# SSD decays: per-head exponentials with a bias on ScalarE and a mask added by Pool, in place of subtractions on VectorE

## The chip, the cores and the metric

One core of one Trainium2 chip runs the whole program. The metric is the device time of one execution in microseconds (us). The engines are named as the profile names them: PE (TensorE, with PEld its weight loads), DVE (VectorE), ACT (ScalarE), POOL (GpSimd) and SP (SyncE, which issues the DMAs).

## The reference, cut to what matters

One layer of a hybrid decoder: an LRU group, a dilated attention group and a Mamba-2 SSD group share an input projection and an output projection. The prompt has 2048 tokens, the sample group 8 sequences of 4 tokens. The change lies in the SSD group, in the decay of a chunk of Q = 128 tokens:

```python
cum = jnp.cumsum(dt * A, axis=2)
seg = cum[:, :, :, None, :] - cum[:, :, None, :, :]
causal = jnp.tril(jnp.ones((Q, Q), dtype=bool))
decay = jnp.exp(jnp.where(causal[None, None, :, :, None], seg, -jnp.inf))
...
scores = jnp.einsum('bcihn,bcjhn->bcijh', Ch, Bh) * decay
y_diag = jnp.einsum('bcijh,bcjhp->bcihp', scores, xdt)
```

There are 16 heads in 2 groups, so 16 chunks times 2 groups of 8 heads, each head with a 128 x 128 matrix of decays.

## The kernel before, in words

The program runs in stages: the input projections, the convolutions, the state of the samples, the attention of the prompt, and last the SSD chunks of the prompt together with the output projection. In this last stage `out_chunk(c)` issues the matmuls of the output projection of chunk c (tile `ops`, L82 to L84, 96 of them for a chunk), and between them the generator `ssd_part(c)` advances the SSD work of a later chunk by steps. The code gives a rough order; the framework's scheduler then fixes the order of the instructions on every engine when the program is built, and at run time each engine goes through its list strictly in order and waits at semaphores.

The SSD work of a chunk has a part for each group g of 8 heads, called here the g=0 part and the g=1 part:

- `ssd_open` (once for a chunk) multiplies B and C on PE (`gp`, L700), and DVE multiplies that with the 0/1 triangle (`gm`, L703). Entries outside the triangle are zero in `gm`.
- `ssd_decay` takes the tile `sg` (128 x 8 heads x 128), which a DMA fills with the row sums `cum` of the chunk, the same in all partitions (L680). There is one such buffer, so the DMA of the next part starts when the matmuls `yd` (L1291) have read this one. ACT first makes `ecB`, exp of the rows, in two pieces (L726). Then DVE subtracts for each head the column sum and caps at 0 (L728, eight instructions of 128 x 128), ACT takes the exponential of all of it (L730, one of 128 x 1024), and DVE multiplies by `gm` (L731, 128 x 1024).
- `ssd_x` turns x on PE (`tpx`, L741), and DVE scales it to `xdt` (L744). POOL multiplies x by D in place (`xb`, L1285) and makes `xte` (L750).
- PE then does `yd` from `sg` and `xdt` (L1291) and `yo` from the state (L1296). DVE sums up y (L1304 to L1307).
- `group_norm`: ACT squares y (`sq`, L757), POOL adds twice (L758, L759), PE sums over partitions (`rs`, L762), ACT makes `rB` (L764, L765), DVE scales y (L766); ACT rounds it to `sh` (L1328) and DVE takes the rest `sl` (L1329). These two are weights of later `ops` matmuls.
- Chunk 0 is prepared ahead, under the last attention unit (`ssd_early`, with buffers `c_`), and chunk 16 is the samples.

ACT and DVE also turn the output chunk into weights (`mh`, L1440, and `ml`, L1441) and finish its rows (`jk`, L1494, `rstd`, `ot`, L1508 and L1509).

Of the kernel before, what the change touches and what calls it, by code (L numbers as in the profile page):

```python
# [8 lines left out]
F32 = mybir.dt.float32  # L9
F32R = mybir.dt.float32r  # L10
AF = mybir.ActivationFunctionType
OP = mybir.AluOpType
# [14 lines left out]
NEG = -1.0e30  # L27
# [5 lines left out]
def tile_hybrid_step(ctx: ExitStack, tc: tile.TileContext, A):  # L33
    nc = tc.nc
    act, dve, pool, pe, sp = nc.scalar, nc.vector, nc.gpsimd, nc.tensor, nc.sync
# [26 lines left out]
    cum = const.tile([128, 17, 16], F32, name="cum")  # L62
# [38 lines left out]
    def softplus_of(pl, out, x, shape, tag):  # L101

        u = pl.tile(shape, F32, tag=tag + "u", name="sp_u")
        dve.tensor_scalar(out=u, in0=x, scalar1=-1.0, scalar2=None, op0=OP.mult)
        dve.tensor_tensor(out=u, in0=u, in1=x, op=OP.min)
        act.activation(out=u, in_=u, func=AF.Exp)
        log1p_of(pl, out, u, shape, tag)
        dve.scalar_tensor_tensor(out=out, in0=x, scalar=0.0, in1=out, op0=OP.max, op1=OP.add)
# [11 lines left out]
    def big(name, n=1024, dt=F32R):  # L120

        if n > 1024:
            return slab.tile([128, n], dt, tag="C", name=name, bufs=8)
        return slab.tile([128, n], dt, tag="A", name=name)
# [327 lines left out]
    with tc.tile_pool(name="dtp", bufs=1) as dp:  # L452

        xx = dp.tile([128, 17, 16], F32, name="xx")
        dve.tensor_tensor(out=xx, in0=dtT, in1=bB[:, None, :].to_broadcast([128, 17, 16]), op=OP.add)
        softplus_of(dp, dtT.rearrange("p c h -> p (c h)"), xx.rearrange("p c h -> p (c h)"), [128, 272], "dt")
        act.activation(out=aB, in_=aB, func=AF.Exp)
        dve.scalar_tensor_tensor(out=xx, in0=dtT, scalar=-1.0, in1=aB[:, None, :].to_broadcast([128, 17, 16]),
                                 op0=OP.mult, op1=OP.mult)
        tr = dp.tile([128, 2, 128], F32, name="tr")  # L460
        sp.dma_start(out=tr[:, 0], in_=A["c_tri"])
        pool.memset(tr[:, 1], 1.0)
        trs = dp.tile([NS, 2, NS], F32, name="trs")
        sp.dma_start(out=trs[:, 0], in_=A["c_tris"])
        sp.dma_start(out=trs[:, 1], in_=A["c_ones"])
        pool.memset(cum[:, 16], 0.0)
        pool.memset(dec[:, 16], 0.0)
        foldT = dp.tile([NS, 128], F32, name="foldT")
        sp.dma_start(out=foldT, in_=A["c_foldT"])
        selh = dp.tile([16, 8, 128], F32, name="selh")  # L470
        sp.dma_start(out=selh, in_=A["c_selh"])
        se = dp.tile([NS, 2, 16], F32, name="se")
        rws = dp.tile([16, 64], F32, name="rws")


        def sums():
            for j, dst in ((0, cum), (1, dec)):
                ps = psA.tile([128, 512], F32, tag="mm", name="cps")
                pe.matmul(ps[:, :256], lhsT=tr[:, j], rhs=xx[:, 0:16].rearrange("p c h -> p (c h)"), start=True, stop=True)
                dve.tensor_copy(out=dst[:, 0:16].rearrange("p c h -> p (c h)"), in_=ps[:, :256])  # L480
                ps = psA.tile([128, 512], F32, tag="mm", name="cps")
                pe.matmul(ps[:NS, :16], lhsT=trs[:, j], rhs=xx[:NS, 16], start=True, stop=True)
                dve.tensor_copy(out=dst[:NS, 16], in_=ps[:NS, :16])
            dve.tensor_tensor(out=tend, in0=dec, in1=cum, op=OP.subtract)
            act.activation(out=tend, in_=tend, func=AF.Exp)
            act.activation(out=dec, in_=dec, func=AF.Exp)
            act.activation(out=se[:, 0], in_=cum[:NS, 16], func=AF.Exp)
            dve.tensor_tensor(out=se[:, 1], in0=tend[:NS, 16], in1=dtT[:NS, 16], op=OP.mult)
            later.append(turn_sums)

        def turn_sums():
            ps = psA.tile([128, 512], F32, tag="mm", name="sps")
            pe.matmul(ps[:, :32], lhsT=foldT, rhs=se.rearrange("t a h -> t (a h)"), start=True, stop=True)
            dve.tensor_copy(out=srep.rearrange("p a h -> p (a h)"), in_=ps[:, :32])
            tp = psT.tile([128, 4, 128], F32, tag="tp", name="tp")
            rw = dp.tile([128, 2, 128], F32, name="rw")
            for g in range(2):
                pe.transpose(tp[:, g], cum[:, 8 * g:8 * g + 8].rearrange("p c h -> p (c h)"), ident)
            pe.transpose(tp[:16, 2, :NS], cum[:NS, 16], ident[:NS, :NS])
            pe.transpose(tp[:16, 3, :NS], dec[:NS, 16], ident[:NS, :NS])  # L500
            dve.tensor_copy(out=rw, in_=tp[:, 0:2])
            sp.dma_start(out=d_cum.rearrange("(g p) t -> p g t", p=128), in_=rw)
            dve.tensor_copy(out=rws.rearrange("p (a t) -> p a t", a=2), in_=tp[:16, 2:4, :NS])
            sp.dma_start(out=d_cums, in_=rws[:, :NS])
            later.append(spread)

        def spread():
            tq = psT.tile([128, 4, 128], F32, tag="tp", name="tq")
            for m in range(8):
                pe.matmul(tq[:, 0, 8 * m:8 * m + 8], lhsT=selh[:, m], rhs=rws[:, NS:64:NL], start=(m == 0), stop=(m == 7),  # L510
                          skip_group_check=True)
            dve.tensor_copy(out=decs.rearrange("p m b -> p (m b)"), in_=tq[:, 0, :64])

        later.append(lambda: later.append(sums))
        q_tile(1)
# [203 lines left out]
    def ssd_decay(c, g, ck, gm, ecB=None):  # L719

        n = TT[c][1]
        sg = load_sg(ck, c, g)
        if ecB is not None:
            for e in range(2):
                pt_ = slice(64 * e, 64 * e + 64)
                act.activation(out=ecB[pt_], in_=sg[pt_].rearrange("p (m e) t -> p e m t", e=2)[:, e], func=AF.Exp)  # L726
        for h in range(8):
            dve.tensor_scalar(out=sg[:n, h], in0=sg[:n, h], scalar1=cum[:n, c, 8 * g + h:8 * g + h + 1],  # L728
                              scalar2=0.0, op0=OP.subtract, op1=OP.min)
        act.activation(out=sg[:n], in_=sg[:n], func=AF.Exp)  # L730
        dve.tensor_tensor(out=sg[:n], in0=sg[:n], in1=gm[:n, g:g + 1].to_broadcast([n, 8, n]), op=OP.mult)  # L731
        return sg

# [505 lines left out]
    late = {}  # L1239

    def ssd_early():

        def piece(t, o, m, n=128):
            return t[:, o:o + m * n].rearrange("p (m t) -> p m t", m=m)

        c_ = [big(f"c0{i}", XC, F32) for i in range(8)]
        bc, tri0 = piece(c_[0], 0, 4), c_[7][:, 512:640]
        sp.dma_start(out=bc, in_=d_xbc[1024:, 0:128].rearrange("(m p) t -> p m t", p=128))
        sp.dma_start(out=tri0, in_=A["c_tri"])
        early[(0, "bc")], late["tri0"] = bc, tri0  # L1250
        ck0.own = {"gm": [piece(c_[0], 512, 2)], "bt": [piece(c_[0], 768, 2)], "xdt": [piece(c_[2], 512, 8, 64), piece(c_[3], 0, 8, 64)]}
        for g in range(2):
            sg, xb = piece(c_[(1, 6)[g]], 0, 8), piece(c_[(2, 7)[g]], 0, 4)
            sp.dma_start(out=xb, in_=d_xbc[512 * g:512 * g + 512, 0:128].rearrange("(m p) t -> p m t", p=128))
            sp.dma_start(out=sg, in_=d_cum[8 * g:8 * g + 8][None].to_broadcast([128, 8, 128]))
            early[(0, "sg", g)], early[(0, "xb", g)] = sg, xb
        for g in range(2):
            ym, zt = piece(c_[5], 512 * g, 4), piece(c_[4], 512 * g, 4)
            sp.dma_start(out=ym, in_=d_y[512 * g:512 * g + 512, 0:128].rearrange("(m p) t -> p m t", p=128))
            sp.dma_start(out=zt, in_=d_z[512 * g:512 * g + 512, 0:128].rearrange("(m p) t -> p m t", p=128))  # L1260
            early[(0, "ym", g)], early[(0, "zt", g)] = ym, zt
# [104 lines left out]
    for i in range(16):  # L1366
# [3 lines left out]
        n = [0, 0]  # L1370
# [31 lines left out]
    ck = es.enter_context(tc.tile_pool(name="ck", bufs=2))  # L1402
    c1 = es.enter_context(tc.tile_pool(name="c1", bufs=1))
# [6 lines left out]
    hT = c1.tile([128, 2, 512], F32, name="hT")  # L1410
    tri = c1.tile([128, 128], F32, name="tri")
    sp.dma_start(out=tri, in_=A["c_tri"])

    ps6 = {"t": (psT, "tp"), "y": (psA, "mm")}
    late.update(ck=ck, ps6=ps6, tri=tri, hT=hT)
    ck0.pool = ck
    ys_ = c1.tile([128, 16, NS], F32, name="ys_")

# [228 lines left out]
```

## Time and profile before

| what | value |
|---|---|
| median of 3 runs | 1945.99 us (1943.85 to 1949.44) |
| profiled execution, its own time | 1949.98 us |
| profiled execution, its span | 1948.2 us |
| PE busy | 1898.8 us, 97% of the span |
| DVE busy | 1065.3 us, 55% |
| ACT busy | 779.6 us, 40% |
| POOL busy | 269.6 us, 14% |

The profiled execution took 3.99 us more than the median of the runs, and 1.8 us of its time lie outside its span. Busy shares are means over stages that differ; the rows below are from the last stage, where the change is. A row of a timeline gives the start in us, the duration in us, engine, line, operation, the tile written and the tiles read, and in square brackets how long the engine stood idle before it and what ended that.

### The profile page before, as it was taken

To read this page: it belongs to the slowest core of one execution; us is meant where nothing else is said; L and a number is where in the kernel's file an instruction comes from. 1 tells how busy PE (TensorE), PEld (TensorE's weight loads), DVE (VectorE), ACT (ScalarE), POOL (GpSimd) and SP (SyncE) were. 2 spreads that over 40 slices of the span, in tenths; PEclk is the share of its full clock that TensorE was granted. 3 is DMA by queue.
4 is the path that set the end of the run, shared out by engine and by line. 5 is a ranking of instruction groups with operands and counts; after the bars stand their busy time and mean duration, and the time that the engine had idled before them with its cause. 6 is when DMAs were issued, how large, how long until landed. Compare 5 with 4: busy or idle time off the path is not lost.

```text
span 1948.2 us, 35823 instructions
## 1 busy us (share of the span) xinstructions
PE 1898.8 (97%) x14178; PEld 1561.5 (80%) x14178; DVE 1065.3 (55%) x2338; ACT 779.6 (40%) x1530; POOL 269.6 (14%) x346
## 2 busy tenths in 40 slices
PE   7999999999999999999999999999998999999998
PEld 7998888888888888887787776777766877677876
DVE  7414444444432666665322226666687776667774
ACT  6411636363622222223233426555654333334332
POOL 0100011111110111111000000000022223222231
PEclk9999999999999999998999999999999999999999
DMA  7422121122223222224577753343375443434442
GB/s 235 129 80 72 44 68 49 61 66 66 69 80 98 72 71 70 79 66 122 150 203 204 204 176 108 116 141 97 114 223 152 125 134 121 118 113 130 126 140 65
DMA packets 278388, 222.03 MB, mean 114 GB/s; under 512 B 34738, under 2 KB 234402, under 8 KB 278220
## 3 DMA queue, kind: packets, MB, share of 16 engines
q1 hardware_dynamic: 278220, 219.73, 37.6%
q8 instruction: 112, 1.84, 0.4%
q14 instruction: 56, 0.46, 0.1%
HBM read 150.81 MB, written 68.86 MB: 113 GB/s over the span
## 4 chain that ended last, share of the span: by engine, by line
PE 83%; ACT 5%; DMA 4%; DVE 4%; issue 2%; SPq 1%; POOL 1%; DVEq 0%; ACTq 0%; POOLq 0%
PE mm L82 15%; PE mm L84 15%; PE mm L83 15%; PE ops L84 5%; PE ops L83 5%; PE ops L82 5%; PE pt L1172 3%; PE o L1208 2%; ACT sr L1144 2%; PE s L1117 2%; PE yd L1291 2%; PE yo L1296 1%; PE s L1096 1%; PE mmt L82 1%; DMA x<-in_x_prompt_dram 1%
## 5 line engine op out<-in xcount | busy, mean ns | idle before, releaser
L82 PE MATMUL mm<-xh,wh 128*128 128x512 f32 (+2 forms) x1600 | 564.6, 353 | 2.3 <-ACT wh L147 1.5
L83 PE MATMUL mm<-xl,wh 128*128 128x512 f32 (+2 forms) x1600 | 562.3, 351 | 0.0
L84 PE MATMUL mm<-xh,wl 128*128 128x512 f32 (+2 forms) x1600 | 561.7, 351 | 0.0
L82 PEld LDWEIGHTS mm<-xh,wh 128*128 128x128 f32 x1600 | 302.3, 189 | 44.6 <-issue 4.3
L84 PEld LDWEIGHTS mm<-xh,wl 128*128 128x128 f32 x1600 | 301.5, 188 | 40.5 <-DVE om L970 1.7
L83 PEld LDWEIGHTS mm<-xl,wh 128*128 128x128 f32 x1600 | 302.1, 189 | 37.3 <-issue 0.2
L146 POOL TENSOR_TENSOR wr<-wr,gC 128x1024 f32<-128x1024 f32 x40 | 79.3, 1982 | 432.5 <-DMA wr<-in_w_in_dram 334.6
L443 DVE SCALAR_TENSOR_TENSOR o<-u,ssdc,o 128x512 f32<-128x512 f32 (+1 forms) x216 | 130.3, 624 | 5.1
L1144 ACT ACTIVATE sr<-sr,nm 128x384 f32<-128x384 f32 (+3 forms) x128 | 97.9, 770 | 23.3 <-DVE nm L1140 18.7
L650 ACT ACTIVATE o<-o 128x512 f32<-128x512 f32 (+2 forms) x60 | 33.1, 552 | 149.2 <-DVE o L443 77.1
L148 DVE SCALAR_TENSOR_TENSOR wl<-wr,wh 128x1024 fp32r<-128x1024 f32 x40 | 49.0, 1225 | 79.6 <-ACT wh L147 79.4
L1055 ACT COPY ptsb<-pt 128x512 f32<-128x512 f32 x96 | 52.4, 583 | 74.8 <-PE pt L1172 74.7
L82 PE MATMUL mmt<-wh,xh 128*128 128x256 f32 (+3 forms) x272 | 79.1, 293 | 1.0 <-ACT xh L254 0.6
L728 DVE TENSOR_SCALAR sg<-sg,cum 128x128 f32<-128x128 f32 (+1 forms) x256 | 72.3, 342 | 13.6 <-ACT ecB L726 13.5
L84 PE MATMUL mmt<-wh,xl 128*128 128x256 f32 (+3 forms) x272 | 78.3, 289 | 0.0
L83 PE MATMUL mmt<-wl,xh 128*128 128x256 f32 (+3 forms) x272 | 77.9, 288 | 0.1
L1172 PE MATMUL pt<-ident,sr 128*128 128x128 f32 x576 | 75.2, 281 | 2.6 <-ACT sr L1144 1.8
L1172 PEld LDWEIGHTS pt<-ident,sr 128*128 128x128 f32 x576 | 63.6, 143 | 14.9 <-issue 8.7
L423 ACT COPY u<-mm 128x512 f32<-128x512 f32 (+1 forms) x80 | 39.5, 494 | 89.0 <-PE mm L84 79.7
L441 DVE TENSOR_SCALAR o<-u,ssdc 128x512 f32<-128x512 f32 (+1 forms) x72 | 38.8, 551 | 66.0 <-ACT u L423 57.5
L726 ACT ACTIVATE ecB<-sg 64x512 f32<-64x512 f32 x60 | 37.8, 630 | 88.1 <-DMA sg<-d_cum 70.5
L1121 DVE CUSTOM_DVE_ANT_0 sr<-s,bias 128x128 f32<-128x128 f32 (+3 forms) x128 | 58.7, 486 | 23.4 <-PE s L1117 22.7
(526 smaller groups left out, 3565.4 us busy)
## 6 DMA issues: line engine op xcount, KB each, us to landing
wr<-in_w_in_dram SPq DMA_DIRECT2D x40, 512.0 KB
sg<-d_cum SPq DMA_DIRECT2D x30, 512.0 KB
d_xbc<-o SPq DMA_DIRECT2D x36, 256.0 KB
x<-in_x_prompt_dram SPq DMA_DIRECT2D x32, 256.0 KB
kc<-in_cache_attn_k_dram SPq DMA_DIRECT2D x32, 256.0 KB
vt<-in_cache_attn_v_dram SPq DMA_DIRECT2D x32, 256.0 KB
xres<-in_x_prompt_dram SPq DMA_DIRECT2D x32, 256.0 KB
out_dram<-ot SPq DMA_DIRECT2D x32, 256.0 KB
```

Source lines behind the costliest of these rows:

```text
L82: pe.matmul(out, lhsT=wh, rhs=xh, start=start, stop=False)
L83: pe.matmul(out, lhsT=wh, rhs=xl, start=False, stop=False)
L84: pe.matmul(out, lhsT=wl, rhs=xh, start=False, stop=stop)
L146: pool.tensor_tensor(out=wr, in0=wr, in1=gC[:, :, None].to_broadcast([128, 8, 128]), op=OP.mult)
L148: dve.scalar_tensor_tensor(out=wl, in0=wr, scalar=scale, in1=wh.bitcast(F32), op0=OP.mult, op1=OP.subtract)
L423: act.copy(out=u[:, 3 + t0:3 + t0 + np_], in_=ps[:, :np_])
L443: dve.scalar_tensor_tensor(out=o, in0=v(t), scalar=w[:, t:t + 1], in1=o, op0=OP.mult, op1=OP.add)
L728: dve.tensor_scalar(out=sg[:n, h], in0=sg[:n, h], scalar1=cum[:n, c, 8 * g + h:8 * g + h + 1], scalar2=0.0, op0=OP.subtract, op1=OP.min)
L1055: act.copy(out=out, in_=in_)
L1121: dve.tensor_tensor_reduce(out=sr[e][r][:, :nk], in0=ps[e][:, :nk], in1=bs[:, e, 512 - nk:512], scale=1.0, scalar=NEG, op0=OP.add, op1=OP. ...
L1144: act.activation(out=sr[e][r], in_=sr[e][r], func=AF.Exp, bias=nm[:, e, r:r + 1], accum_out=ll[:, e, r:r + 1])
L1172: pe.transpose(tp[:, r], sr[e][r][:, 128 * g:128 * g + 128], ident)
```

## The change

`cum` is negated once, when it is made (one DVE instruction of 128 x 256). A 128 x 128 tile `neg` is made from the triangle (0 inside, the constant -1e30 outside; `neg0` for chunk 0). In `ssd_decay`, for the chunks 0 to 15, the eight subtractions and the one exponential are replaced: POOL adds `neg` to all eight heads of `sg` (one instruction of 128 x 1024), and ACT takes eight exponentials of 128 x 128, each with the negated column sum of its head as bias. The multiplication by `gm` stays. The samples (c == 16) keep the old way.

```diff
+            dve.tensor_scalar(out=cum[:, 0:16], in0=cum[:, 0:16], scalar1=-1.0, scalar2=None, op0=OP.mult)
...
-        for h in range(8):
-            dve.tensor_scalar(out=sg[:n, h], in0=sg[:n, h], scalar1=cum[:n, c, 8 * g + h:8 * g + h + 1],
-                              scalar2=0.0, op0=OP.subtract, op1=OP.min)
-        act.activation(out=sg[:n], in_=sg[:n], func=AF.Exp)
+        if c == 16:
...
+        else:
+            pool.tensor_tensor(out=sg, in0=sg, in1=late["neg0" if c == 0 else "neg"][:, None, :].to_broadcast([128, 8, 128]),
+                               op=OP.add)
+            for h in range(8):
+                act.activation(out=sg[:, h], in_=sg[:, h], func=AF.Exp, bias=cum[:, c, 8 * g + h:8 * g + h + 1])
         dve.tensor_tensor(out=sg[:n], in0=sg[:n], in1=gm[:n, g:g + 1].to_broadcast([n, 8, n]), op=OP.mult)
...
+        late["neg0"] = c_[7][:, 640:768]
+        pool.tensor_scalar(out=late["neg0"], in0=tri0, scalar1=-1.0, scalar2=-NEG, op0=OP.add, op1=OP.mult)
...
+    neg = c1.tile([128, 128], F32, name="neg")
+    pool.tensor_scalar(out=neg, in0=tri, scalar1=-1.0, scalar2=-NEG, op0=OP.add, op1=OP.mult)
```

What the scheduler makes of it is seen in the lists of the engines. The lines of the changed kernel are some 2 to 13 higher than those of the kernel before (L730 becomes L738, L731 L739, L744 L752, L764 L772, L1328 L1339). ACT, the g=1 part of a chunk late in the last stage, from `ecB` to `sh`, before:

```order
L726 ACTIVATE ecB<-sg 64x512
L757 ACTIVATE sq<-y 128x512
L726 ACTIVATE ecB<-sg 64x512
L730 ACTIVATE sg<-sg 128x1024
L1440 CAST mh<-ym 128x512
L764 ACTIVATE rB<-rs,eps_t 128x128
L765 ACTIVATE rB<-rB 128x128
L1494 ACTIVATE jk,oss<-ops 128x512
L1328 CAST sh<-y 128x512
```

And of the change, the same part:

```order
L728 ACTIVATE ecB<-sg 64x512
L765 ACTIVATE sq<-y 128x512
L728 ACTIVATE ecB<-sg 64x512
L738 ACTIVATE sg<-sg,cum 128x128 x8
L772 ACTIVATE rB<-rs,eps_t 128x128
L1453 CAST mh<-ym 128x512
L773 ACTIVATE rB<-rB 128x128
L1507 ACTIVATE jk,oss<-ops 128x512
L1339 CAST sh<-y 128x512
```

Eight short exponentials stand where the long one stood, and everything behind them keeps its place but for `mh`, which moves behind the first `rB`.

POOL, one part of a chunk (the same for g=0 and g=1), before:

```order
L1285 TENSOR_TENSOR xb<-xb,dF 128x512
L750 TENSOR_TENSOR xte<-xdt,tend 128x512
L1320 TENSOR_TENSOR hT<-hT,dec 128x512
L758 TENSOR_TENSOR sq<-sq 128x256
L759 TENSOR_TENSOR sq<-sq 128x128
```

And of the change:

```order
L1296 TENSOR_TENSOR xb<-xb,dF 128x512
L758 TENSOR_TENSOR xte<-xdt,tend 128x512
L1331 TENSOR_TENSOR hT<-hT,dec 128x512
L766 TENSOR_TENSOR sq<-sq 128x256
L767 TENSOR_TENSOR sq<-sq 128x128
L735 TENSOR_TENSOR sg<-sg,neg 128x1024
```

The addition of the mask comes last, behind the two additions of `group_norm`, which belong to the part before.

DVE, the g=1 part from `ml` to `xdt`, before:

```order
L1441 TENSOR_TENSOR ml<-ym,mh 128x512
L728 TENSOR_SCALAR sg<-sg,cum 128x128 x8
L1321 TENSOR_TENSOR hT<-hT,stp 128x512
L731 TENSOR_TENSOR sg<-sg,gm 128x1024
L1441 TENSOR_TENSOR ml<-ym,mh 128x512
L766 TENSOR_TENSOR y<-y,rB 128x512
L1329 TENSOR_TENSOR sl<-y,sh 128x512
L744 TENSOR_TENSOR xdt<-tpx,dtT 128x512
```

And of the change:

```order
L1454 TENSOR_TENSOR ml<-ym,mh 128x512
L1332 TENSOR_TENSOR hT<-hT,stp 128x512
L739 TENSOR_TENSOR sg<-sg,gm 128x1024
L774 TENSOR_TENSOR y<-y,rB 128x512
L1454 TENSOR_TENSOR ml<-ym,mh 128x512
L1340 TENSOR_TENSOR sl<-y,sh 128x512
L752 TENSOR_TENSOR xdt<-tpx,dtT 128x512
```

The subtractions are gone, the second `ml` and `y<-y,rB` have changed places, and `xdt` is still last. PE's list differs in the first chunks of this stage; from the `yd` of chunk 2, g=1, to the end it is the same, instruction by instruction.

## Rows read from the trace of the kernel before

**Rows 1.** Busy by stage: stretch, length, PE, PEld, DVE, ACT, POOL, PEclk, DMA

```profile
1430.00:1500.00 70.00, 62.67 (x322) 45.31 (x319) 56.84 (x101) 34.89 (x63) 18.19 (x18) 0.98 0.62 183
1500.00:1915.00 415.00, 410.84 (x2327) 319.80 (x2327) 289.32 (x558) 150.74 (x313) 120.08 (x137) 1.00 0.41 124
```

**Rows 2.** Waits of PEld, 1500 to 1915 us: us in total, times, longest

```profile
PEld yd L1291 <- DVE xdt L744: 9.5, 18, 1.9
```

**Rows 3.** Timeline of DVE, g=1 part of one chunk

```profile
1813.96 2.33 DVE L728 TENSOR_SCALAR sg<-sg,cum 128x128 f32<-128x128 f32 x8
...
1817.48 1.23 DVE L731 TENSOR_TENSOR sg<-sg,gm 128x1024 f32<-128x1024 f32 x1 [0.56 <-ACT sg L730]
1818.62 0.68 DVE L1441 TENSOR_TENSOR ml<-ym,mh 128x512 fp32r<-128x512 f32 x1
1819.22 0.68 DVE L766 TENSOR_TENSOR y<-y,rB 128x512 f32<-128x512 f32 x1
1820.59 0.69 DVE L1329 TENSOR_TENSOR sl<-y,sh 128x512 fp32r<-128x512 f32 x1 [0.69 <-ACT sh L1328]
1821.20 0.69 DVE L744 TENSOR_TENSOR xdt<-tpx,dtT 128x512 f32<-128x512 f32 x1
```

**Rows 4.** Timeline of ACT, the same part

```profile
1814.19 0.63 ACT L726 ACTIVATE ecB<-sg 64x512 f32<-64x512 f32 x1
1816.38 1.06 ACT L730 ACTIVATE sg<-sg 128x1024 f32<-128x1024 f32 x1 [1.56 <-DVE sg L728]
1817.35 0.60 ACT L1440 CAST mh<-ym 128x512 fp32r<-128x512 f32 x1
1817.86 0.36 ACT L764 ACTIVATE rB<-rs,eps_t 128x128 f32<-128x128 f32 x1
1818.25 0.31 ACT L765 ACTIVATE rB<-rB 128x128 f32<-128x128 f32 x1
...
1819.94 0.62 ACT L1328 CAST sh<-y 128x512 fp32r<-128x512 f32 x1
```

**Rows 5.** Timeline of POOL, the same part

```profile
1814.24 0.79 POOL L758 TENSOR_TENSOR sq<-sq 128x256 f32<-128x256 f32 x1 [2.65 <-ACT sq L757]
1815.11 0.51 POOL L759 TENSOR_TENSOR sq<-sq 128x128 f32<-128x128 f32 x1
1821.01 1.18 POOL L1285 TENSOR_TENSOR xb<-xb,dF 128x512 f32<-128x512 f32 x1 [5.39 <-PE tpx L741]
```

**Rows 6.** Timeline of PE, the end of the same part

```profile
1821.69 0.39 PE L83 MATMUL ops<-wo11l,sh 128*128 128x512 f32 x1
1821.92 0.39 PE L84 MATMUL ops<-wo11h,sl 128*128 128x512 f32 x1
1822.24 1.09 PE L1291 MATMUL yd<-sg,xdt 128*64 128x128 f32 x16
```

**Rows 7.** Timelines of POOL, DVE and PE, the g=0 part that follows

```profile
1829.17 0.46 POOL L759 TENSOR_TENSOR sq<-sq 128x128 f32<-128x128 f32 x1
...
1837.00 0.68 DVE L744 TENSOR_TENSOR xdt<-tpx,dtT 128x512 f32<-128x512 f32 x1
...
1838.27 1.09 PE L1291 MATMUL yd<-sg,xdt 128*64 128x128 f32 x16
```

**Rows 8.** One line by itself: POOL L146, ns min/median/max, first and last start

```profile
L146 POOL TENSOR_TENSOR wr<-wr,gC x40: 1895/1897/2341, 54.9 to 1121.7; 128x1024 f32<-128x1024 f32 x40
```

**Rows 9.** Groups by line and shape, ACT, 1160 to 1430 us: busy, mean ns

```profile
L1144 ACT ACTIVATE sr<-sr,nm 128x768 f32<-128x768 f32 x32 | 29.7, 935 | 14.1 <-DVE nm L1140 9.5 <-issue 4.6
...
L1144 ACT ACTIVATE sr<-sr,nm 128x384 f32<-128x384 f32 x32 | 19.3, 610 | 2.4 <-DVE nm L1140 2.4
```

**Rows 10.** Timelines of POOL and DVE, a stretch where both work in SBUF

```profile
1576.39 1.04 POOL L1285 TENSOR_TENSOR xb<-xb,dF 128x512 f32<-128x512 f32 x1 [6.04 <-PE tpx L741]
...
1576.57 1.94 DVE L731 TENSOR_TENSOR sg<-sg,gm 128x1024 f32<-128x1024 f32 x1 [0.54 <-ACT sg L730]
```

**Rows 11.** Timeline of DVE, where chunk 0 is prepared

```profile
1413.91 0.68 DVE L728 TENSOR_SCALAR c<-c,cum 128x128 f32<-128x128 f32 x3 [5.21 <-DMA c<-d_cum]
```

More of the change, by code (lines that the diff above doesn't have):

```diff
@@ L726, in ssd_decay @@
                 act.activation(out=ecB[pt_], in_=sg[pt_].rearrange("p (m e) t -> p e m t", e=2)[:, e], func=AF.Exp)
-        for h in range(8):
-            dve.tensor_scalar(out=sg[:n, h], in0=sg[:n, h], scalar1=cum[:n, c, 8 * g + h:8 * g + h + 1],
-                              scalar2=0.0, op0=OP.subtract, op1=OP.min)
-        act.activation(out=sg[:n], in_=sg[:n], func=AF.Exp)
+        if c == 16:
+            for h in range(8):
+                dve.tensor_scalar(out=sg[:n, h], in0=sg[:n, h], scalar1=cum[:n, c, 8 * g + h:8 * g + h + 1],
+                                  scalar2=0.0, op0=OP.subtract, op1=OP.min)
+            act.activation(out=sg[:n], in_=sg[:n], func=AF.Exp)
+        else:
+            pool.tensor_tensor(out=sg, in0=sg, in1=late["neg0" if c == 0 else "neg"][:, None, :].to_broadcast([128, 8, 128]),
+                               op=OP.add)
+            for h in range(8):
+                act.activation(out=sg[:, h], in_=sg[:, h], func=AF.Exp, bias=cum[:, c, 8 * g + h:8 * g + h + 1])
         dve.tensor_tensor(out=sg[:n], in0=sg[:n], in1=gm[:n, g:g + 1].to_broadcast([n, 8, n]), op=OP.mult)
@@ L1412, in tile_hybrid_step @@
     sp.dma_start(out=tri, in_=A["c_tri"])
+    neg = c1.tile([128, 128], F32, name="neg")
+    pool.tensor_scalar(out=neg, in0=tri, scalar1=-1.0, scalar2=-NEG, op0=OP.add, op1=OP.mult)
     ps6 = {"t": (psT, "tp"), "y": (psA, "mm")}
-    late.update(ck=ck, ps6=ps6, tri=tri, hT=hT)
+    late.update(ck=ck, ps6=ps6, tri=tri, hT=hT, neg=neg)
     ck0.pool = ck
```

## The prediction

> **What bounds the kernel now.** I looked first at the busy times by stage. In the last stage, 1500 to 1915 us, PE is busy 410.8 of 415 us; DVE is busy 70% of it, ACT 36%, POOL 29% [rows 1]. So PE is the bound, and a cheaper instruction on another engine gives nothing by itself: at most 4.2 us of PE's idle time can be won here. The waits of PE come next: what PE waits for in this stage is `xdt`, 18 times, 9.5 us in total at the weight loads [rows 2], some of which the running matmuls cover. So the side work is finished just in time for PE, twice in a chunk. Anything that makes the side work later than it is stops PE, and as PE's list is fixed, such a stop is paid in full in every chunk.
>
> Then I read the timelines of one chunk to see what `xdt` waits for. In the g=1 part DVE makes the eight subtractions, ACT's exponential ends at 1816.38 + 1.06 = 1817.44, DVE multiplies at 1817.48, and `ml`, `y`, `sl` and `xdt` follow in DVE's list [rows 3, 4]. `xdt` has nothing to do with the decays but stands behind them in the queue. It ends at 1821.88. PE starts a matmul every 0.23 us, is free for `yd` at 1821.92 + 0.23 = 1822.15, and starts it at 1822.24 [rows 6]. The slack is about 0.3 us. In the g=0 part `xdt` ends at 1837.68 and `yd` starts at 1838.27, a slack of 0.5 to 0.6 us [rows 7].
>
> **What the change takes away.** In each part DVE loses 2.33 us of subtractions [rows 3] and ACT loses 1.06 us of exponential [rows 4]. The DVE time is worth nothing directly, as DVE waits later in the same list for the exponential (0.56 us) and for `sh` (0.69 us) [rows 3]. The negation of `cum` and the making of `neg` happen once or twice; I cost them at zero, under the projections and the end of attention. If that cover were gone they would cost an instruction each, under 1 us.
>
> **What it adds, on POOL.** One addition of 128 x 1024. The nearest row is POOL's own multiplication of that size with a broadcast operand: 1.90 us [rows 8]. DVE's two-operand instruction of this size is 1.23 us [rows 3], the lower bound; 2.34, the longest of rows 8, the upper. I take 1.90, the same engine and shape. [...]
>
> **What it adds, on ACT.** Eight exponentials of 128 columns with a bias from SBUF instead of one of 1024. ACT's exponentials with such a bias take 935 ns at 768 columns and 610 at 384 [rows 9]: 0.85 ns for a column, so 128 columns are 610 - 256 x 0.85 = 393 ns, call it 0.40 us. Neighbours overlap: the exponential ends at 1817.44 and the next starts at 1817.35 [rows 4], 0.09 us. So the start of one follows the other after 0.31, and eight take 7 x 0.31 + 0.40 = 2.57 us. The bounds: 0.27 each, as a 0.36 us instruction with bias would give [rows 4], 2.25 us; without overlap 3.2 us.
>
> **The g=1 part replayed with these prices.** POOL's list has the addition behind the two additions of `sq`, which end at 1815.11 + 0.51 = 1815.62 [rows 5]; `ecB` has been read by 1814.82 [rows 4] and does not count. From one POOL instruction to the next there are 0.08 us, so the addition runs from 1815.70 to 1817.60. The exponentials run from 1817.65 to 1820.22, where the old one ended at 1817.44: 2.8 us later. Behind them on ACT stand `rB`, `mh` and `sh`. `rB`'s two instructions with `mh` between them now end near 1821.2, just before DVE wants them.
>
> DVE multiplies from 1820.26 and its next instruction, `y<-y,rB`, can follow after 1.14 us, at 1821.40 [rows 3]. Here POOL comes in again. Its `xb` is ready at 1821.01 [rows 5], behind `tpx`, while DVE's multiplication is running. What such an overlap does is in another place: `xb` starts at 1576.39, DVE's multiplication 0.18 us later, and the latter takes 1.94 instead of 1.23 us; it ends 1.08 us after `xb` has [rows 10]. The other way round, `xb` met a running `sl`, took 1.18 instead of 1.04, and ended 0.91 us after it [rows 3, 5, 10]. So POOL and a DVE instruction with two operands in SBUF take turns, and the one that came second goes on when the first is done. [...]
>
> In the g=1 part `xb` will be the one that waits when DVE's multiplication ends, and `y<-y,rB` comes next, so I let `xb` go first: 0.9 us, and `y` starts at 1822.3. `y` to `sh` to `sl` to `xdt` then keep their old distances (`y` 1819.22 to the end of `xdt` 1821.88, 2.66 us [rows 3]; the second `ml` now fits into the wait for `sh`): `xdt` ends at 1822.3 + 2.66 = 1824.96, and `yd` starts 0.08 later, at 1825.04 instead of 1822.24. PE stands 2.8 us. Without the turn for `xb` it is 1.9.
>
> **The g=0 part.** `sq` ends at 1829.63 [rows 7], the addition at 1831.61, and the exponentials with `rB` among them near 1834.7, `rB` at 1834.4. Then `y` 0.60, `gm` (half as wide, at most the same 0.60), the multiplication 1.14, `sl` 0.61 and `xdt` 0.68 from 1834.45 end at 1838.08 at the latest, 0.2 before `yd` starts now [rows 3, 7]. No stall. The old exponential stood late in ACT's list here, so there was room.
>
> **The sum.** PE's list is the same from chunk 2, g=1, to the end: 14 g=1 parts. 14 x 2.8 = 39 us. The opening of the stage, 1430 to 1500, has 70 - 62.7 = 7.3 us of idle PE [rows 1] and another order of instructions; it can win those 7.3 or lose 2 x 2.8 = 5.6 in the two parts of chunk 1; I take 0. Under the attention, chunk 0's subtractions no longer hold up DVE for 5.2 us until a DMA lands [rows 11]; instead POOL's addition (1.9 us) and then ACT wait for the same DMA, with attention's copies behind. Between +1.9 and -5.2, I take 0, as the same data end the wait. Against the profiled execution: 1949.98 + 39.2 = 1989.2. That execution stands 3.99 us above the median of the runs, so the prediction is 1985 us, 2.0% slower.
>
> **The rivals.** Two runs of this kernel that differ by less than about 0.3% (6 us) can't be told apart; that is the bound used here.
>
> *No turn for `xb`.* DVE's instructions follow one another without a gap, and `xb` waits until DVE pauses. For it: the eight short subtractions run in 2.33 us with two POOL instructions beside them, so something gave way only a little [rows 3, 5]. Against it: rows 10. Then 14 x 1.9 = 27 us, 1973 us.
>
> *Nothing to see.* The addition and the exponentials come out so that PE's slack covers them. They would have to be finished by about 1818.3, 0.3 us of slack plus the 0.6 us for which DVE now waits for `sh` behind the 1817.44 of today: 2.6 us for both from 1815.70, against the 4.5 that I find. That needs an addition below 1 us and exponentials near 0.2. Time 1940 to 1952.
>
> *Faster.* The gain is in the start of the stage: DVE freed from the 5.2 us wait for chunk 0's DMA and from 2.33 us per part, so that the first weights `sl` and `xdt` come earlier and PE's 7.3 us idle time goes. 7.3 + about 2 of the 5.2 is 9 us, 1937 us. It decides only if the g=1 stalls stay under 9 / 14 = 0.6 us each.
>
> *The exponentials don't overlap.* 0.40 each: 0.6 us more per part, so 3.4 in g=1 and up to 0.3 in g=0, 14 x 3.7 = 52 us, 1998 us.
>
> **How the numbers follow.** Forecast with the turn for `xb`, own range 1977 to 1993: 0.44. No turn, 1965 to 1980: 0.28. Nothing to see: 0.13. Faster: 0.10. No overlap: 0.05. The predicted time is the forecast's, 1985. Below 1948 lies the faster case and most of the one with nothing to see, under 0.2; 2000 takes in the last one. Faster by over 0.3%: 0.10; within: 0.13; slower: 0.77.
>
> **What the profile after would show.** Right: waits of PE's `yd` for `xdt` of 2 to 3 us in every g=1 part and almost none in g=0; POOL's addition at 1.9 us right behind `sq`; eight exponentials 0.31 apart; DVE waiting before its multiplication by `gm` some 2 us longer than now; PE's idle time in the stage higher by about 39 us. Wrong in the size: a `y<-y,rB` that starts right behind the multiplication while `xb` is stretched (no turn). Wrong in the cause: `yd` waiting for `sg` itself, or for a DMA. The prediction falls if the addition runs well below 1.9 us, or if PE's idle time in this stage stays near 4 us.

## The result and the profile after

The changed kernel takes 2018.41 us (median of 3 runs, 2015.97 to 2020.94), before it was 1945.99: the ratio is 1.0363, with a 95% interval from 1.0344 to 1.0382. It is 72 us slower. The profiled execution has a span of 2014.2 us, 66.0 more than before; 64.9 of that arises behind 1453 us, where the chunks 1 to 15 run.

The answer to [rows 1], the busy times by stage (stretch, length, then busy time and count of PE, PEld, DVE, ACT and POOL, the granted clock of PE as a share of its full speed, DMA share, GB/s):

```profile
1430.00:1500.00 70.00, 60.07 (x306) 43.73 (x305) 51.91 (x66) 34.45 (x75) 24.62 (x20) 0.95 0.58 174
1500.00:1915.00 415.00, 376.92 (x2034) 292.01 (x2032) 219.68 (x307) 165.17 (x444) 165.66 (x145) 0.95 0.37 112
```

PE was busy 410.8 of 415 us before, now 376.9. It stands 38 us in this stretch, and DVE is busy 70 us less. The column to look at is PEclk: 0.95 in both stretches, where it was 0.98 and 1.00.

What PE waited for, 1500 to 1980 us (us in total, times, longest us):

```profile
PE yd L1302 <- DVE xdt L752: 39.6, 13, 3.5
PE rs L770 <- POOL sq L767: 3.8, 4, 2.3
```

One g=1 part of the changed kernel, timelines of POOL, ACT, DVE and PE one after the other (start, us, engine, line, operation, tiles, and in brackets the idle time before and what ended it), to be read against [rows 3 to 6]:

```profile
1826.66 0.46 POOL L767 TENSOR_TENSOR sq<-sq 128x128 f32<-128x128 f32 x1
1827.07 2.38 POOL L735 TENSOR_TENSOR sg<-sg,neg 128x1024 f32<-128x1024 f32 x1
1832.60 1.56 POOL L1296 TENSOR_TENSOR xb<-xb,dF 128x512 f32<-128x512 f32 x1 [3.15 <-PE tpx L749]
...
1829.48 2.45 ACT L738 ACTIVATE sg<-sg,cum 128x128 f32<-128x128 f32 x8 [3.13 <-POOL sg L735]
...
1832.04 1.22 DVE L739 TENSOR_TENSOR sg<-sg,gm 128x1024 f32<-128x1024 f32 x1 [3.52 <-ACT sg L738]
1833.18 1.53 DVE L774 TENSOR_TENSOR y<-y,rB 128x512 f32<-128x512 f32 x1
...
1836.00 0.68 DVE L752 TENSOR_TENSOR xdt<-tpx,dtT 128x512 f32<-128x512 f32 x1
...
1833.51 0.39 PE L84 MATMUL ops<-wo11h,sl 128*128 128x512 f32 x1
1836.83 1.28 PE L1302 MATMUL yd<-sg,xdt 128*64 128x128 f32 x16 [2.93 <-DVE xdt L752]
1838.04 2.08 PE L1307 MATMUL yo<-bc,hT 128*128 128x128 f32 x8
```

Read it along the chain. `sq` ends at 1827.12, and the addition follows at once and ends at 1829.45. The eight exponentials end at 1831.93, and DVE multiplies at 1832.04, after an idle time of 3.52 us. `y<-y,rB` meets `xb` on POOL and takes 1.53 us in place of 0.68. `xdt` ends at 1836.68, and PE, whose last matmul ended at 1833.90, starts `yd` at 1836.83: a stop of 2.93 us.

Then look at the row of `yo`: eight matmuls take 2.08 us. In the kernel before, behind the `yd` of [rows 6], they took 1.16:

```profile
1823.26 1.16 PE L1296 MATMUL yo<-bc,hT 128*128 128x128 f32 x8
```

The granted clock of the stop, of the matmuls behind it and of those after that (columns as above):

```profile
1834.00:1836.80 2.80, 0.00 (x0) 0.00 (x0) 2.60 (x4) 0.62 (x1) 0.20 (x2) 1.00 0.09 18
1837.80:1841.00 3.20, 3.20 (x15) 2.76 (x12) 0.81 (x2) 0.00 (x0) 0.80 (x2) 0.50 0.43 163
1842.00:1845.00 3.00, 3.00 (x15) 2.46 (x15) 1.34 (x3) 2.02 (x5) 1.02 (x2) 1.00 0.58 156
```

While PE stands, the row still shows 1.00; within one microsecond after it has begun again the clock is at 0.50 of its full speed, for at least the 3.2 us of the second row, and 1.00 again in the third. So the stop costs its 2.93 us and then some 1.6 us more (3.2 x (1 - 0.50)).

**Where the 66.0 us are.** I compared the starts of `yd` in the two traces, part by part. At the g=1 part of chunk 2 the changed kernel is 7.49 us behind, at the g=1 part of chunk 15 it is 64.86 behind, and 1.1 us more come after it. Between the two lie 57.4 us: PE stops of 39.6 us for `xdt` in 13 parts, less 2.4 us of such stops that the kernel before has here too, and 20.1 us of half clock (the sum of busy time x (1 - granted clock) over windows of one us, 1544 to 1946 us). That makes 57.3. The account is not as exact as that looks: six matmuls (`wo12h,sl` to `wo14l,sh`, 1.4 us) that the kernel before runs behind the `yd` of chunk 2, g=1, run ahead of it in the changed kernel; but for these, PE's two lists are the same from there on. Counted by equal work some 6 us lie ahead of this `yd` and some 59 between the two, of which 1 to 2 us have no place in the sum.

The first 7.5 us lie between the `yd` of chunk 0, where the two kernels are 0.1 us apart, and that of chunk 2, g=1. Timelines of POOL and PE there:

```profile
1462.56 2.37 POOL L735 TENSOR_TENSOR sg<-sg,neg 128x1024 f32<-128x1024 f32 x1 [4.32 <-ACT ecB L728]
1464.89 1.17 POOL L766 TENSOR_TENSOR sq<-sq 128x256 f32<-128x256 f32 x1
1466.14 0.94 POOL L767 TENSOR_TENSOR sq<-sq 128x128 f32<-128x128 f32 x1
...
1467.13 0.49 PE L770 MATMUL rs<-sq,ones 128*128 128x128 f32 x2 [3.39 <-POOL sq L767]
```

Here the scheduler put the addition ahead of `sq` in POOL's list, and PE waits 3.39 us for `sq`, where it waited 0.54 before. The addition is not shown to be the whole cause. ACT's part of `sq`, which POOL needs, ends only at 1463.66, and e1 and e9 below wait 2.10 and 2.78 us at the same place without an addition on POOL. In e9 the opening is no shorter than here; in e1, which has no addition in these chunks at all, its loss goes. What makes the opening late stays open.

### The profile page after: what moved, and what is told of

Its sections match the earlier page's. It is cut to its first block, busy times and chain, and to the rows that moved or that the text cites. A ratio compares the mean times of both kernels' runs of the same rounds, so it can differ in the third digit from the quotient of the medians.

```text
span 2014.2 us, 35874 instructions
## 1 busy us (share of the span) xinstructions
PE 1922.3 (95%) x14178; PEld 1579.0 (78%) x14178; DVE 1019.5 (51%) x2083; ACT 820.1 (41%) x1754; POOL 352.6 (18%) x380
## 4 chain that ended last, share of the span: by engine, by line
PE 73%; ACT 8%; DVE 6%; DMA 5%; POOL 3%; issue 3%; SPq 1%; DVEq 0%; POOLq 0%; ACTq 0%
PE mm L82 14%; PE mm L84 14%; PE mm L83 14%; PE ops L82 3%; PE ops L83 3%; PE ops L84 3%; ACT sr L1152 3%; PE pt L1180 2%; POOL sg L735 2%; ACT sg L738 2%; PE yd L1302 2%; PE s L1125 2%; DMA sg<-d_cum 2%; PE o L1216 2%; PE yo L1307 2%
## 5 line engine op out<-in xcount | busy, mean ns | idle before, releaser
L84 PEld LDWEIGHTS mm<-xh,wl 128*128 128x128 f32 x1600 | 300.5, 188 | 39.6 <-issue 1.0
L146 POOL TENSOR_TENSOR wr<-wr,gC 128x1024 f32<-128x1024 f32 x40 | 79.3, 1984 | 429.2 <-DMA wr<-in_w_in_dram 378.9
L738 ACT ACTIVATE sg<-sg,cum 128x128 f32<-128x128 f32 x240 | 77.0, 389 | 67.3 <-POOL sg L735 67.3
L1302 PE MATMUL yd<-sg,xdt 128*64 128x128 f32 x480 | 40.6, 319 | 40.7 <-DVE xdt L752 39.6
L735 POOL TENSOR_TENSOR sg<-sg,neg 128x1024 f32<-128x1024 f32 x30 | 72.0, 2400 | 20.2 <-ACT ecB L728 20.1
```

Source lines behind the costliest of these rows:

```text
L84: pe.matmul(out, lhsT=wl, rhs=xh, start=False, stop=stop)
L146: pool.tensor_tensor(out=wr, in0=wr, in1=gC[:, :, None].to_broadcast([128, 8, 128]), op=OP.mult)
L735: pool.tensor_tensor(out=sg, in0=sg, in1=late["neg0" if c == 0 else "neg"][:, None, :].to_broadcast([128, 8, 128]), op=OP.add)
L738: act.activation(out=sg[:, h], in_=sg[:, h], func=AF.Exp, bias=cum[:, c, 8 * g + h:8 * g + h + 1])
L1302: pe.matmul(yd[64 * e:64 * e + 64, m], lhsT=xdt[:, 2 * m + e], rhs=sg[:, 2 * m + e], start=(m == 0), stop=(m == 3), skip_group_check=True)
```

## The experiments

The theory after the traces: the addition on POOL lengthens the chain from `sq` to `xdt` in the g=1 part; PE stops there, and each stop brings a stretch at half clock. The rivals are named in the expectations: the lower clock has another cause (A), the eight exponentials are the cost (B), or POOL's work beside DVE is the cost wherever it lies (C). A fourth, D, belongs to e9: DVE gets too much work.

| run | edit | median us | ratio to before, 95% interval |
|---|---|---|---|
| e1_no_add | change without the addition | 1945.46 | 1.0002 [0.9988, 1.0015] |
| e2_one_exp | change with one exponential | 1978.34 | 1.0164 [1.0144, 1.0184] |
| e3_warm | change with matmuls in PE's stop | 2004.31 | 1.0296 [1.0280, 1.0311] |
| e4_xdt_x6 | before with `xdt` six times | 1966.43 | 1.0110 [1.0090, 1.0130] |
| e5_add_only | before plus the addition | 2014.78 | 1.0357 [1.0329, 1.0385] |
| e6_add_half | change, addition in two halves | 1986.04 | 1.0195 [1.0165, 1.0226] |
| e7_no_xb | change without `xb` on POOL | 1998.28 | 1.0268 [1.0243, 1.0293] |
| e8_g0_only | change in g=0 alone | 1952.04 | 1.0027 [1.0011, 1.0043] |
| e9_dve_add | change, addition on DVE | 1951.87 | 1.0030 [1.0017, 1.0043] |
| e10_g1_only | change in g=1 alone | 2006.22 | 1.0311 [1.0297, 1.0325] |
| e11_x_first | before, `xdt` written first | 1952.47 | 1.0033 [1.0020, 1.0045] |

The time came out in a range that the theory gave for e2, e6 and e9. It missed its range by 0.2 to 2 us in e5, e7, e8 and e10, by 4 to 5 in e11 and e3, by 11 in e1 and by 39 in e4. In the code below, views and broadcasts of the operands are left out.

### The addition, the exponentials, and both

```diff
 e1   -pool.tensor_tensor(out=sg, in0=sg, in1=late[...], op=OP.add)              # c > 0
      -act.activation(out=sg[:, h], in_=sg[:, h], func=AF.Exp, bias=cum[...])
      +act.activation(out=sg[:, h], in_=sg[:, h], func=AF.Exp, bias=dtT[...])    # c > 0
 e2   -for h in range(8): act.activation(out=sg[:, h], ..., bias=cum[...])
      +act.activation(out=sg, in_=sg, func=AF.Exp)
 e5 (in the kernel before, ahead of its subtractions)
      +if 0 < c < 16: pool.tensor_tensor(out=sg, in0=sg, in1=neg, op=OP.add)
```

> The changed kernel without POOL's addition of the mask in chunks 1 to 15 (the mask is left out there, and the bias is dt in place of the column sum, so that the exponentials stay finite; the eight exponentials are the same in number and shape). Theory (the g=1 chain of addition and exponentials makes xdt late, and each stop of PE is followed by a stretch at half clock): the addition's 2.4 us leave the chain, xdt comes 2.5 to 3.4 us earlier, the stop before yd falls from about 3.05 to between 0 and 0.6 us, the granted clock stays at 1.00 from 1550 on, and 55 to 62 us of the 72 come back: 1956 to 1963 us. Rival A (the lower clock has nothing to do with the stops): the stops go but the clock loss of 22 us stays: 1975 to 1982. Rival B (eight exponentials are the cost, the addition lies beside them): stops above 1.5 us stay, over 1990.

> The changed kernel with one exponential of 128 x 1024 in place of the eight (the column sum is left out); POOL's addition stays. Theory: the chain is shorter by 2.2 to 2.5 less 1.06, so 1.1 to 1.4 us; the stop before yd falls from 3.05 to 1.6 to 2.0 us, which is 15 to 20 us back, 1998 to 2003; if the clock no longer falls after stops of that length, another 22 us, 1976 to 1981. Rival A (the clock falls whatever the stops): 1998 to 2003 with clock falls in places that do not follow a stop. Rival B (the exponentials are the whole cost): stops go altogether, below 1965. Rival C (only the addition and its contention with DVE count): 2015 to 2020.

> The kernel before, eight subtractions and one exponential, with POOL's addition of the mask ahead of them in chunks 1 to 15 (the result stays the same). Theory (what counts is POOL's addition in the chain, and stops of PE of over 2 us bring the half clock): the addition ends near 1818.1 of the chunk shown in [rows 3], the subtractions at 1820.4, the exponential at 1821.5 where it was 1817.44, so the stop before yd in g=1 is about 3.8 us; 14 x 3.8 = 53 us and 14 x 1.6 = 22 us of half clock: 2015 to 2035, more if g=0 stops too. Rival B (the eight exponentials are the cost): 1944 to 1955. Rival A (the lower clock belongs to the eight exponentials or to something else of the change): 1998 to 2005, clock 1.00.

Without the addition all 72 us come back, where the theory asked for 55 to 62. It had left the loss of the opening standing, and that goes too: in the profiled run the `yd` of chunk 2, g=1, starts at 1501.36, in the kernel before at 1502.07. DVE's multiplication, in the timeline of e1's DVE, then waits 0.41 us for the eighth exponential, less than the 0.56 us for the one long exponential in [rows 3]:

```profile
1845.82 1.23 DVE L740 TENSOR_TENSOR sg<-sg,gm 128x1024 f32<-128x1024 f32 x1 [0.41 <-ACT sg L739]
```

So eight exponentials by themselves cost nothing that these runs can tell; B falls. Behind an addition they do: with one exponential in their place the stops shrink to 1.21 to 1.35 us in eight parts, in all from 39.6 to 20.3 us, and the time falls by 40 us, twice that, since much of the half clock goes too (behind the stops for `xdt` 4 stretches in place of 11). And the addition alone, put into the kernel before, costs 69 us without any of the eight exponentials. That speaks against A as well: nothing of the change but the addition is in e5, and half clock follows its stops too. The stops lie in part elsewhere than I placed them. Waits of PE in e5, 1500 to 1990 us:

```profile
PE rs L764 <- POOL sq L761: 23.3, 14, 4.1
PE yd L1293 <- DVE xdt L746: 14.4, 12, 2.1
PE yd L1293 <- DVE sg L733: 11.2, 10, 2.5
```

Where the addition stands ahead of `sq` in POOL's list, `rs` waits for `sq`; that is 23.3 us of e5, where the changed kernel has 3.8. So the time lies at the edge of the expected range, but not by the stops of 3.8 us in every g=1 part that were to make it. Of e5's eight stops of 1.97 to 2.52 us from 1520 us on, five brought a stretch at half clock.

### The clock behind a stop

```diff
 e3   +for _ in range(12 if g == 1 and c > 1 else 0):
      +    pe.matmul(yd, lhsT=wo[0][0][:, 0:128], rhs=wo[0][0][:, 0:512], start=True, stop=True)
 e4 (in the kernel before)
      -dve.tensor_tensor(out=xdt, in0=xv, in1=dtT[...], op=OP.mult)
      +for _ in range(6 if g == 1 and 1 < c < 16 else 1):
      +    dve.tensor_tensor(out=xdt, in0=xv, in1=dtT[...], op=OP.mult)
```

> The changed kernel with 12 more matmuls of 128 x 512 right ahead of yd in the g=1 parts of chunks 2 to 15, into yd's own PSUM tile and overwritten by yd; they need nothing that is late, so they run while PE would stand (12 x 0.227 = 2.7 us). Theory: xdt is as late as before, PE's wait shrinks to some 0.3 us, yd starts at the same distance, but the granted clock stays at 1.00 and its 22 us come back: 1993 to 1999. Rival A (the clock falls for another reason than the stop): the clock loss stays, 2015 to 2022.

> The kernel before, with its subtractions and its one exponential, in which DVE computes xdt six times in place of once in the g=1 parts of chunks 2 to 15 (the same result). 5 x 0.68 = 3.4 us later, less the slack of 0.3: a stop of 3.1 us before yd, without POOL's addition or the eight exponentials. Theory: the stops cost 14 x 3.1 = 43 us and the stretch at half clock behind each 1.6 us more, 20 us: 2005 to 2012. Rival A (the lower clock belongs to the change, not to the stop): 1987 to 1991, and a clock of 1.00.

In e3 the 12 matmuls run where PE stood, and `yd` starts after a wait of 0.2 to 1.0 us. PE's timeline:

```profile
1830.42 2.88 PE L1301 MATMUL yd<-wo0h 128*128 128x512 f32 x12
1833.57 1.09 PE L1304 MATMUL yd<-sg,xdt 128*64 128x128 f32 x16 [0.27 <-DVE xdt L752]
```

And the windows view behind this `yd` (columns as above):

```profile
1834.50:1838.00 3.50, 3.50 (x23) 2.97 (x20) 2.07 (x3) 0.00 (x0) 1.09 (x2) 1.00 0.55 190
```

From 1510 us on PE loses nothing to half clock, where the changed kernel lost 21.8 us to it; the opening loses 5.1 us, 2.1 more than there. The time falls by 14.1 us and ends 5 us above the expected range. `xdt` is late as before, so A is out for the stage's chunks: the same late work without a stop of PE does not lower the clock. Two things keep the rest. The 12 matmuls also run in chunks 2 and 8, where the changed kernel had no stop for `xdt`, and cost some 2.7 us each there. And there are new short waits: from 1500 to 1980 us `tpx` waits 4.2 us for `bt`, 0.3 in the changed kernel.

e4 missed: it did not make the stop that it was to make. DVE's `xdt` takes 4.31 us for six, but PE has no wait in front of `yd`. Its timeline there (the view ends at 1869 us, so three of the 16 matmuls of `yd` are not in it):

```profile
1867.97 0.39 PE L84 MATMUL ops<-wo0h,ml 128*128 128x512 f32 x1
1868.32 0.95 PE L1292 MATMUL yd<-sg,xdt 128*64 128x128 f32 x13
```

The scheduler allowed for DVE's longer work and set `yd` behind `wo0h,ml`, 15 matmuls later than behind `wo11h,sl`, as in [rows 6]. 15 x 0.23 = 3.4 us, about what the five copies take, 4.31 - 0.69 = 3.6. So a wait that the order foresees was filled with other matmuls, while in the changed kernel PE's list from chunk 2, g=1, on is the old one but for the six matmuls named above, and nothing fills the wait. The run costs 20 us, of which 13.4 are 13 waits of `rs` for `sq`, none over 1.3 us. It has no half clock there, but on the clock behind a long stop it tells nothing.

The stops themselves tell more. Those of over 1 us that PE made for `xdt` from 1525 us on in five traces, by length, with the number that a stretch at 0.5 followed:

| trace | stops, us | followed by half clock |
|---|---|---|
| changed kernel | 12 of 2.92 to 3.55, one of 1.48 | 11, not behind 1.48 and one of 3.25 |
| e10_g1_only | 12 of 2.92 to 3.23 | 12 |
| e7_no_xb | 12 of 2.02 to 3.01, one of 1.05 | 8, not behind 1.05 |
| e6_add_half | 7 of 1.92 to 2.90, 5 of 1.72 to 1.78 | 5, all in the first group |
| e2_one_exp | 4 of 2.32 to 3.33, 8 of 1.21 to 1.35 | 4, all in the first group |

Two stretches of e2 show both ends, each behind a `yd` that had waited, 2.46 us and 1.21 us (columns as above):

```profile
1673.00:1675.00 2.00, 2.00 (x15) 1.67 (x12) 0.00 (x0) 0.00 (x0) 0.18 (x1) 0.50 0.06 20
1815.90:1819.00 3.10, 3.10 (x20) 2.70 (x19) 1.75 (x3) 0.00 (x0) 1.10 (x2) 1.00 0.50 179
```

In this table a stretch began between 1.3 us before PE started again and 1.5 us after. It isn't a sharp edge, and length alone does not decide: the changed kernel's stop of 3.25 us went without it, as did those of 3.39 us at 1467 and 2.32 us at 1505, which are for `sq` and so not in the table. In e8 a half clock came behind a stop of 1.17 us, and in the opening of the kernel before behind two of 1.23 and 0.55 us, 1.7 us apart. What else decides stays open.

### The length of the chain, and xb's turn

```diff
 e6   -pool.tensor_tensor(out=sg, in0=sg, in1=neg, op=OP.add)              # 128 x 1024
      +for q in range(2):
      +    pool.tensor_tensor(out=sg[:, 4 * q:4 * q + 4], ..., op=OP.add)  # 128 x 512
 e7   -pool.tensor_tensor(out=xb, in0=xb, in1=dF[...], op=OP.mult)         # c > 0
 e9   -pool.tensor_tensor(out=sg, in0=sg, in1=neg, op=OP.add)
      +dve.tensor_tensor(out=sg, in0=sg, in1=neg, op=OP.add)
```

> The changed kernel with the addition of the mask in two halves of four heads, so that ACT can begin with the first heads some 1.2 us earlier; all the work stays. Theory (the length of the chain from sq to xdt is what counts): xdt comes 1.1 to 1.2 us earlier, the stop in g=1 falls from 3.05 to about 1.9; 14 x 1.15 = 16 us back, and between none and all of the 22 us of half clock: 1980 to 2002. Rival C (POOL's work beside DVE is the cost, wherever it lies): 2014 to 2022.

> The changed kernel without POOL's multiplication of x by D in chunks 1 to 15 (it is left out, x is added unscaled). Theory with the turn for xb: y<-y,rB starts right behind DVE's multiplication, 0.9 us earlier; the stop falls to about 2.15 us; 14 x 0.9 = 13 us back, the half clock mostly stays: 2000 to 2008. Rival (xb costs DVE no time on this path): 2015 to 2021.

> The changed kernel with the addition of the mask on DVE in place of POOL; all else stays, and the result too. Theory (length and place of the addition are the cost): on DVE it does not stand behind sq, begins when the second ecB has been read (1814.82 in the chunk of [rows 4]) and takes 1.23 us; the exponentials end near 1818.6 in place of 1820.2, DVE's multiplication is some 1.1 us later than before the change, the slack and xdt's place ahead of sl cover it: no stop over 1 us, clock 1.00, 1944 to 1956. Rival B (the eight exponentials cost by themselves behind any addition): 1975 to 1990. Rival D (DVE's extra 1.23 us in each part make DVE late): 1960 to 1980.

e6 lies where the theory put it: the same work on POOL, 32 us less, so C falls as the whole of the cost. ACT begins behind the first half (in one g=1 part the two additions run from 1809.01 to 1811.54 and the exponentials start at 1810.32), and the stops shrink to 1.7 to 2.9 us. e7 shows the turn for `xb`. DVE's timeline of e7:

```profile
1819.63 1.23 DVE L739 TENSOR_TENSOR sg<-sg,gm 128x1024 f32<-128x1024 f32 x1 [3.49 <-ACT sg L738]
1820.77 0.69 DVE L774 TENSOR_TENSOR y<-y,rB 128x512 f32<-128x512 f32 x1
```

`y<-y,rB` takes 0.69 us, in the changed kernel 1.53: 0.84 us a part. The run is 20 us faster: the stops for `xdt` sum up to 28.9 us where they were 39.6, and the half clock to 19.3 where it was 24.8 (opening included).

e9 is the repair: the addition on DVE takes 1.23 us and doesn't stand behind `sq` on POOL. DVE's timeline in a g=1 part of e9:

```profile
1819.08 1.23 DVE L735 TENSOR_TENSOR sg<-sg,neg 128x1024 f32<-128x1024 f32 x1 [0.94 <-ACT ecB L728]
...
1823.08 1.23 DVE L739 TENSOR_TENSOR sg<-sg,gm 128x1024 f32<-128x1024 f32 x1 [2.06 <-ACT sg L738]
```

The waits of PE in e9, 1500 to 1990 us:

```profile
PE rs L770 <- POOL sq L767: 5.2, 5, 2.1
PE yd L1302 <- DVE xdt L752: 2.3, 2, 1.3
```

The multiplication still waits 2.06 us for the exponentials, but `xdt` is late only twice. 1951.87 us is 6 us above before. In the profiled run these lie in the opening: at the `yd` of chunk 2, g=1, e9 is 6.7 us behind, at the end of the span 5.4; it loses some 5 us there to half clock, before 1.7. Of D, which asked for 1960 to 1980 us, nothing is to be seen.

### The two parts, and an idea for both kernels

```diff
 e8   -if c == 16:
      +if c == 16 or (g == 1 and c > 0):     # e10: g == 0; the subtraction adds the negated cum
 e11 (in the kernel before)
      -sg = ssd_decay(c, g, ck, gm, ecB)
      -yield
       xb, xdt, xte = ssd_x(c, g, ck, ps6)
      +sg = ssd_decay(c, g, ck, gm, ecB)
      +yield
```

> The change in the g=0 parts alone (and in chunk 0); the g=1 parts of chunks 1 to 15 subtract the column sum on VectorE as before. Theory (g=0 has the slack for it): no stop before yd, clock 1.00, 1943 to 1950, no difference to before. Rival (each part pays alike, half of the 72 us): 1975 to 1988.

> The change in the g=1 parts alone (and in chunk 0); the g=0 parts of chunks 1 to 15 subtract the column sum on VectorE as before. Theory (the whole cost lies in g=1): 2008 to 2020, as with the whole change. Rival (g=0's lateness adds to it): 1980 to 2000.

> The kernel before with the call that makes xdt written ahead of the call that makes the decays. PE turns x 6 rows earlier, and xdt stands ahead of sl in DVE's list. Theory (PE is the bound; its waits for xdt are at most a few us in all): 1940 to 1948, at best 5 us better. Rival (xdt's place in DVE's list holds more than PE's waits show): below 1938. Other side (an earlier tpx takes PSUM or PE's time from the output projection): 1950 to 1960.

The change in the g=1 parts alone (e10) costs 60 of the 72 us, 2 us below the expected range, and in the g=0 parts alone (e8) 6, 2 us above it. Waits of PE in e8, 1500 to 1990 us:

```profile
PE tpx L749 <- ACT bt L712: 2.4, 5, 0.9
...
PE yd L1302 <- DVE xdt L752: 0.9, 1, 0.9
```

And in e10:

```profile
PE yd L1302 <- DVE xdt L752: 35.9, 12, 3.2
```

e11 takes PE's waits for `xdt` away altogether and brings nothing: 1952.47 us, 6 slower, in the range that the expectation gave to its other side. Its profiled execution has a span of 1948.5 us, as good as before's 1948.2, so the trace can't tell where the 6 us are; that stays open. No version beats the kernel before, and e1 says why: with an addition that costs nothing the change comes out at 1945.46, since what it saves is DVE's time, and PE is the bound.

## Why the prediction was wrong

**PE is the bound, and DVE's saved time is worth nothing.** Right. DVE does 46 us less over the span, and e1, which keeps the saving without the addition, stands at 1.0002.

**The replay of the g=1 part.** Right in its mechanism and near in size for one part: 12 stops of 2.92 to 3.55 us in g=1 parts where it said 14 of 2.8. That the sum, 39.6 us with the one stop of 1.48 in a g=0 part, so nearly meets the 39 forecast is in part luck: chunks 2 and 8 have no stop for `xdt`, and the others are longer than forecast. Counted from the end of `sq`, the addition ends after 2.33 us (forecast 1.98), the exponentials after 4.81 (4.60), `xdt` after 9.56 (9.34). `xb`'s turn is 0.84 us (0.9), and in e7, without it, the stops are 10.7 us shorter in all, where 13 were forecast.

**The addition's price, 1.90 us.** Mis-sized. The page of the changed kernel (busy us, mean ns, then idle before):

```profile
L738 ACT ACTIVATE sg<-sg,cum 128x128 f32<-128x128 f32 x240 | 77.0, 389 | 67.3 <-POOL sg L735 67.3
...
L735 POOL TENSOR_TENSOR sg<-sg,neg 128x1024 f32<-128x1024 f32 x30 | 72.0, 2400 | 20.2 <-ACT ecB L728 20.1
```

2.40 us a piece, 0.50 more than the multiplication of [rows 8] that I took as the nearest row, and above the longest of those, the upper bound. Against DVE's addition in e9 it is 2.40 / 1.23 = 1.95 times as long; [rows 8] over DVE's 1.23 in [rows 3] had given 1.90 / 1.23 = 1.54. The exponentials were priced at 0.40 us each and take 0.389; eight take 2.45 where 2.57 was said. The two errors partly cancel.

**"Such a stop is paid in full in every chunk."** This is the step that failed. It is paid with more than its length: 11 of the 13 stops are followed by a stretch at a granted clock of 0.50, 20.1 us that no term of the sum held. These 20 us are the larger part of what the forecast lacked; the opening below is the other. The kernel before has a sign of it that I read past: in the opening, where PE stands 7.3 us, its granted clock was 0.98 [rows 1]. e3 shows that filling the stop keeps the clock (nothing lost to half clock from 1510 us on, against 21.8 us); e2, that no half clock follows its 8 stops of 1.21 to 1.35 us. What sets the clock beyond that, no run shows.

**The g=0 part, no stop.** Nearly right: one stop of 1.48 us in chunk 3, none after it, and e8 costs 6 us.

**The opening, 0 in bounds of -7.3 and +5.6.** Wrong: +7.5 us, beyond the bound. I gave POOL's list the addition behind `sq` everywhere; in chunk 1 it stands ahead of it, and `rs` waits. How much of the 7.5 that makes is not shown. The attention ahead of it, also taken at 0, was right: 0.1 us.

The sum again, against the profiled execution before: 1948.2 + 7.5 + 37.2 + 20.1 + 1.1 = 2014.1, and the span is 2014.2 (to 1 or 2 us, as said above). Of the added 65.9 us the forecast had 39.2. Of the rivals, no turn for `xb`, nothing to see and faster did not occur, nor did exponentials without overlap.

## What to carry to other kernels

Where PE is the bound, price a stop of PE at its length and, for stops as long as these (12 of 2.92 to 3.55 us, one of 1.48), at the half clock that 11 of the 13 brought: here 3.05 us on average cost some 4.6. Before moving work to a slower engine that is idle on average, look at what stands ahead of it in that engine's list and at what its result releases: the same addition took 2.40 us a piece on POOL and 1.23 on DVE, and cost 72 us on POOL and 6 on DVE, though DVE was the busier of the two. If a late result can't be helped, let PE have other matmuls there, as the scheduler did in e4.

## What the hardware showed that I had not expected

Among PE's stops for `xdt` in the five traces, 40 of 47 of 1.92 to 3.55 us came with a stretch of 3 to 7 us at half clock, and none of 15 of 1.05 to 1.78; stops outside that table break both sides of it. A POOL addition of 128 x 1024 with its second operand repeated over the middle dimension takes 2.40 us, POOL's multiplication of the same size in [rows 8] 1.90; two additions of half the size take 2.53 together. Whether the operation or the form of the repeated operand makes the difference, no run tells.
